# A hybrid attention and recurrence encoder step: bias rows reversed through DRAM instead of by a matmul, wider memsets on GpSimd, and the last softmax scalings on VectorE or ScalarE

## The chip, the cores and the metric

The kernel runs on one core of a Trainium2 chip, in a single launch. The metric is the device time of that launch in microseconds, the median of several runs. The engines are TensorE (PE, matmuls), VectorE (DVE), ScalarE (ACT), GpSimd (POOL) and SyncE (SP, whose queue issues every DMA of this kernel). Each engine works through its own list of instructions in a fixed order and waits for the others by semaphores.

## The reference

One layer of an encoder that has two kinds of heads side by side, for a prompt of 2048 rows and a sample of 64 rows with a cache. One input projection makes eight kinds of features. Four pairs of attention heads use q, k, v and a gate; four recurrent heads use q, f, i and a gate. The attention adds a learned bias by clipped relative distance:

```python
idx = jnp.clip(rel, -REL_CLIP, REL_CLIP) + REL_CLIP          # REL_CLIP = 128
bias = rel_bias[:, idx].astype(jnp.float32)
s = jnp.einsum('bnqhd,bnkhd->bnhqk', q, k).astype(jnp.float32) * ATTN_SCALE + bias
s = jnp.where(valid[None, :, None], s, NEG_INF)
p = jax.nn.softmax(s, axis=-1).astype(v.dtype)
return jnp.einsum('bnhqk,bnkhd->bnqhd', p, v)
```

A chunk of 64 rows attends to itself and the eight chunks before it, so for 128 query rows a tile of bias is 128 x 640 and its entry depends on the difference of column and row alone: each row is the row above it, shifted by one. The first 384 columns all lie beyond the clip and hold one number per head; the last 256 hold the shifted rows. After both branches comes the output projection with the residual and a final norm.

## The kernel before

The rows are cut into four blocks (SUPER): 512, 512 + 64 (the sample), 512 and 512. For every block TensorE runs 32 projection jobs, one per kind and head, of 24 or 48 matmuls `acc<-xh,w` and `acc<-xl,w`: inputs and weights are held as a high and a low part, and three products are summed. Between those matmuls the kernel weaves the attention of the pairs (scores `s`, transposes `tr`, products `pv`), the recurrence of the heads (bank `g`) and, near the end, the output products `acc<-...,slot`. In block 0 each weight is also loaded (`wraw`), split by VectorE and GpSimd into `w` and stored to `wd`, from where the later blocks load it.

The order is not written out by hand. A planner (class Plan, lines 52 to 237) runs the parts of the program as threads at build time and keeps a clock for each engine from a table of costs (Queue.cost, lines 284 to 330). A thread yields what it waits for, a condition, a time, or a time on an engine, and goes on when the planned clock is there. `C.pick(t, D=..., A=...)` names the engine on which work that is ready at t would be done first by those clocks. For SP the planner counts 520 ns from a DMA's start, then its bytes at 370 per ns behind what is already on the way, then 2000 ns and a lag of 100 (lines 204 to 208, 236 to 237, 288). The instructions then stand in that order on each engine whatever the real times are.

The bias of a pair is made once, in block 0, by `load_bias` (line 815), in a single buffer `bias` of 128 x 2 x 640, and stored to `biasd` for the later blocks. A DMA loads a window `ck` in which row p starts at element p of the reversed bias; the rows then run in the wrong direction, so a float32 matmul with the constant `flip` (ones on the other diagonal) turns them over into bank `g`, and VectorE negates the result into `nb[:, :, 384:640]`. VectorE fills the first 384 columns from `far` (`bias<-reset,far`), and two memsets put a large number where a key is not to be seen. The store to `biasd` follows, and `d.bias_at` lets the pair's scores begin (softmax_rows, line 1013). A softmax is: scores on TensorE into the single bank `s`; one custom VectorE instruction that adds the bias and takes the minimum (`pr,nm<-s,bias`, with its row `nm`; the order calls both ISA); the exponential on ScalarE with its sum; a reciprocal; and the scaling of the probabilities. The scaling is on VectorE, except once `parts` is in `have`, which is so only in the last pair of the last block: there it is on ScalarE (line 1049). The probabilities are then transposed and split into `ph`, a high part by ScalarE and a low part by VectorE, for the `pv` products.

GpSimd gets a short memset of `C.breath`, a tile of its own, after three instructions that the planner queued behind one another (lines 261 to 265); its result is not used.

Of the kernel before, what the change touches and what calls it, by code (L numbers as in the profile page):

```python
# [8 lines left out]
F32 = mybir.dt.float32  # L9
# [3 lines left out]
ALU = mybir.AluOpType  # L13
# [4 lines left out]
P = 128  # L18
D = 1024
# [353 lines left out]
def hymba_step(  # L373
# [24 lines left out]
    C = Plan()  # L398
    act, dve, pool, pe, sp = (Queue(C, e, x) for e, x in (("A", nc.scalar), ("D", nc.vector), ("P", nc.gpsimd),
                                                          ("T", nc.tensor), ("S", nc.sync)))  # L400
# [4 lines left out]
    cst = ctx.enter_context(tc.tile_pool(name="cst", bufs=1))  # L405
    wk = ctx.enter_context(tc.tile_pool(name="wk", bufs=2))
    dr = ctx.enter_context(tc.tile_pool(name="dr", bufs=1, space=DRAM))
# [5 lines left out]
    def T(pool_, shape, dt, tag, **kw):  # L413
        uid[0] += 1
        C.name(homes.get(id(pool_), ""), tag, kw.get("bufs") or 1, f"{tag}_{uid[0]}")
        return pool_.tile(list(shape), dt, tag=tag, name=f"{tag}_{uid[0]}", **kw)

    def psum(tag, shape=(P, 512), bufs=1):
        return T(ps, shape, F32, tag, bufs=bufs)
# [22 lines left out]
    def mm32(out, w, x):  # L442
        pe.matmul(out, w, x, start=True, stop=True)

    tk = {k: Tok(C, n) for k, n in dict(acc=2, s_ps=1, tr=2, pv=1, g=1, pr=PRB, ph=2, sig=2, vT=2, mixa=2,
                                     w=WBUFS, raw=RAWB, xn=XNB, kv=1, q=1, sga=2, bias=1, gf=1, gi=1, gg=1,
                                     ck=1, slot=4, x4=0, x5=0, rec=1).items()}
# [1 line left out]

    ident = T(cst, [P, P], F32, "ident")  # L450
    make_identity(nc, ident)
    flip = T(cst, [P, P], F32, "flip")
    ones = T(cst, [P, P], F32R, "ones")
    mask = T(cst, [P, P], U32, "mask")
    eps_t = T(cst, [P, 1], F32, "eps")
    one_t = T(cst, [P, 1], F32, "one")
    C.breath = T(cst, [P, 1], F32, "breath")
    reset = T(cst, [P, 512], F32, "reset")
    asb = [T(cst, [P, 4, P], F32, f"asb{i}") for i in range(2)]
    g_norm = T(cst, [P, NHB], F32, "gnorm")  # L460
# [5 lines left out]
    have = set()  # L466

    def constants():
        pool.memset(eps_t, EPS)
        pool.memset(one_t, 1.0)  # L470
        maskf = asb[0][:, 0]
        pool.memset(maskf, 1.0)
        dve.tensor_copy(ones, maskf)
        pool.memset(flip, 1.0)
        pool.affine_select(out=flip, in_=flip, pattern=[[1, P]], compare_op=ALU.is_equal, fill=0.0,
                           base=-(P - 1), channel_multiplier=1)
        pool.affine_select(out=maskf, in_=maskf, pattern=[[1, P]], compare_op=ALU.is_ge, fill=0.0,
                           base=0, channel_multiplier=-1)
        dve.tensor_copy(mask, maskf)
        pool.memset(reset, 1.0)  # L480
        pool.memset(reset.rearrange("p (b t) -> p b t", t=32)[:, :, 0:1], 0.0)
        pool.memset(asb[0], 0.0)
# [333 lines left out]
    def load_bias(sb, p, d):  # L816
        yield from tk["bias"].get()
        nb = d.bias = T(wk, [P, 2, 640], F32, "bias", bufs=1)
        if sb:
            sp.dma_start(nb, biasd[p])  # L820
            d.bias_at = C.dma(655)
            return
        yield from tk["ck"].get()
        win = T(wk, [P, 4, P], F32, "ck", bufs=1).rearrange("p (h a) c -> p h (a c)", h=2)
        sp.dma_start(win, bass.AP(rel_rev.tensor, 2 * p * 383, [[1, P], [383, 2], [1, 256]]))
        far = T(wk, [P, 2], F32, "far", bufs=1)
        sp.dma_start(far, bass.AP(rel_rev.tensor, 2 * p * 383, [[0, P], [383, 2]]))
        t = C.dma(400)
        yield "D", t
        for h in range(2):  # L830
            dve.tensor_scalar(nb[:, h, 0:384], reset[:, :384], 0.0, far[:, h : h + 1], ALU.mult, ALU.subtract)
        C.dve(600)
        yield from tk["g"].get()
        pw = psum("g")
        pe.matmul(pw, flip, win.rearrange("p h c -> p (h c)"), start=True, stop=True)
        tk["ck"].put()
        t = C.pe()
        yield "D", t
        dve.tensor_scalar(nb[:, :, 384:640], pw.rearrange("p (h c) -> p h c", h=2), -1.0, None, ALU.mult)
        tk["g"].put(1, C.dve())  # L840
        dve.memset(nb[64:128, :, 0:64], BIG)
        dve.memset(nb[0:64, :, 576:640], BIG)
        t = C.dve(900, t)
        d.bias_at = t
        yield t
        sp.dma_start(biasd[p], nb)
        C.dma(655)
# [38 lines left out]
    def pair_jobs(sb, p):  # L886
# [10 lines left out]
        def open_():  # L897

            yield from tk["kv"].get()
            d.kd = T(pa, [P, 2, WIN + NMAX], F32R, "kd")  # L900
            d.v = T(pa, [P, 9, 4, 64], F32R, "v")
            d.q = T(pa, [P, 2, QW], F32R, "q")
            if sb:
                cd = carry[sb - 1][p]
                sp.dma_start(f32(d.kd[:, :, 0:512]), cd[:, 0:2, :])
                sp.dma_start(f32(d.v[:, 0:4].rearrange("p t s d -> p (t s d)")),
                             cd[:, 2:4, :].rearrange("p a c -> p (a c)"))
                d.k_t = d.v_t = C.dma(1024)
            C.spawn(load_bias(sb, p, d), 1)
            if smp:  # L910
                pool.memset(f32(d.v[DEC:, 4 + WIN // P]), 0.0)
                C.spawn(sample_cache(d), 1)
# [98 lines left out]
    def softmax_rows(d, h, qc, spans, bcol, nk, out):  # L1011

        yield lambda: d.q_n >= qc + P and d.k_n >= qc + P and d.bias_at is not None
        yield max(d.q_t, d.k_t, d.bias_at) + 300.0
        yield from tk["s_ps"].get()
        yield from tk["pr"].get()
        sps = s_ps()
        for part in (d.q, ql):
            for i, (k0, kn) in enumerate(spans):
                mm(sps[:, i, :kn], part[:, h, qc : qc + P], d.kd[:, h, k0 : k0 + kn], kn,  # L1020
                   start=part is d.q, stop=part is ql)
        t = C.pe()
        yield "D", t
        s = T(wk, [P, 640], F32, "pr", bufs=PRB)
        nm = T(wk, [P, 2], F32, "nm", bufs=4)
        ns, kn = len(spans), spans[0][1]
        dve.tensor_tensor_reduce(
            s[:, :nk].rearrange("p (a c) -> p a c", a=ns), sps[:, :ns, :kn],
            d.bias[:, h, bcol : bcol + nk].rearrange("p (a c) -> p a c", a=ns),
            1.0, 3e38, ALU.add, ALU.min, nm[:, 0:1])  # L1030
        t = C.dve(nk + 80, t)
        tk["s_ps"].put(1, t)
        d.left -= 1
        if d.left == 0:
            if d.sb == len(SUPER) - 1 and d.p == NPAIR - 1:
                have.add("scores")
                tk["x4"].put()
            tk["bias"].put()
        yield "A", t
        yield from softmax_exp(s, nm, nk, out, t)  # L1040

    def softmax_exp(s, nm, nk, out, t):
        sm = T(wk, [P, 1], F32, "sm", bufs=4)
        act.activation(s[:, :nk], s[:, :nk], AF.Exp, bias=nm[:, 0:1], scale=-1.0, accum_out=sm)
        t = C.act(nk + 300, t)
        yield "D", t
        dve.reciprocal(sm, sm)
        t = C.dve()
        if "parts" in have:
            yield "A", t  # L1050
            act.activation(s[:, :nk], s[:, :nk], AF.Copy, scale=sm)
            t = C.act()
        else:
            dve.tensor_scalar(s[:, :nk], s[:, :nk], sm, None, ALU.mult)
            t = C.dve()
        out.append((s, t))
# [184 lines left out]
    def sample_a(d, c0, marks):  # L1241
# [41 lines left out]
        yield "A", t  # L1283
        out = []
        yield from softmax_exp(s, nm, 576, out, t)
        pr, t = out[0]
        yield lambda: marks[-1]["pv"] and turn["ph"] == turn["given"]
# [749 lines left out]
    def program():  # L2037


        dve.memset(g_in, 0.0)  # L2040
        constants()
        kroom = f32(T(pa, [P, 2, WIN + NMAX], F32R, "kd")).rearrange("p a c -> p (a c)")
        vroom = f32(T(pa, [P, 9, 4, 64], F32R, "v")).rearrange("p t s d -> p (t s d)")
# [252 lines left out]
```

## Time and profile before

| what | us |
|---|---|
| median of 3 runs (1261.01 to 1264.11) | 1261.85 |
| the profiled execution | 1260.86 |
| its span in the trace | 1259.00 |
| TensorE busy in it | 1238.8 |
| VectorE, ScalarE, GpSimd busy | 891.9, 706.9, 379.9 |

The profile is of one execution. Busy time of an engine counts its instructions, not its waits; TensorE's matmuls overlap, so a matmul's own duration is longer than the step from one to the next. A tile's view lists the instructions that write or read it with the shortest, middle and longest duration in ns. A wait row reads: who waited, for whose work on which tile, microseconds in total, times, the longest. A row of the timeline has the start, the length, the engine and the work, and in brackets the idle time just before with what ended it. For a DMA, "to landing" is the time from its issue to the arrival of its last piece.

### The profile page before, as it was taken

How to read it: one execution, taken by the hardware profiler on the slowest of the kernel's cores; microseconds unless marked ns; L12 is line 12 of the kernel's file. 1: busy time of each engine (PE TensorE's matmuls, PEld its weight loads, DVE VectorE, ACT ScalarE, POOL GpSimd, SP SyncE). 2: the span in 40 equal slices, each digit the busy share in tenths (PEclk: the TensorE clock that was granted, in tenths of full speed). 3: DMA queues.
4: the chain of work that ended last, by engine and by line, in shares of the span. 5: the costliest groups of instructions: out<-in, count | busy, mean ns of one | idle time of the engine just before them, and what ended most of it. 6: DMA issues, size and time to landing. Idle time of an engine off the chain costs nothing. (4 is left out here: it accounts for less than half of the span.)

```text
span 1259.0 us, 22201 instructions
## 1 busy us (share of the span) xinstructions
PE 1238.8 (98%) x8120; PEld 1081.6 (86%) x8120; DVE 891.9 (71%) x1854; ACT 706.9 (56%) x1548; POOL 379.9 (30%) x703
## 2 busy tenths in 40 slices
PE   9999999999999999999999999999999999999997
PEld 8788887999999999998888888998888888788786
DVE  7786968766857678686584849783838574578886
ACT  6453546665656557575565656764636454753443
POOL 7766655111120210202533634110101104451110
PEclk9999999999999999999999999999999999999999
DMA  7887787645354554636879597646454657886331
GB/s 288 301 288 244 247 282 281 219 168 202 138 188 142 181 200 144 216 125 236 272 248 303 206 364 254 220 164 210 144 212 136 222 178 279 324 277 203 126 134 67
DMA packets 94830, 271.72 MB, mean 216 GB/s; under 512 B 10305, under 2 KB 43073, under 8 KB 77058
## 3 DMA queue, kind: packets, MB, share of 16 engines
q1 hardware_dynamic: 94722, 270.31, 61.4%
q8 instruction: 64, 1.05, 0.3%
q14 instruction: 44, 0.36, 0.1%
HBM read 186.66 MB, written 83.62 MB: 215 GB/s over the span
## 5 line engine op out<-in xcount | busy, mean ns | idle before, releaser
L266 PE MATMUL acc<-xh,w 128*128 128x512 f32 (+2 forms) x2720 | 568.4, 348 | 1.0 <-ACT sig L266 0.8
L266 PEld LDWEIGHTS acc<-xh,w 128*128 128x128 f32 x2720 | 436.7, 189 | 51.7 <-issue 1.4
L266 PE MATMUL acc<-xl,w 128*128 128x512 f32 (+2 forms) x1360 | 297.4, 348 | 0.0
L266 PEld LDWEIGHTS acc<-xl,w 128*128 128x128 f32 x1360 | 219.3, 189 | 24.9 <-issue 0.5
L266 POOL TENSOR_TENSOR mixa<-mixa,sga 128x256 f32<-128x256 f32 (+1 forms) x36 | 29.8, 828 | 334.8 <-DVE mixa L266 259.6
L266 DVE CUSTOM_DVE_ANT_0 pr<-s,bias 128x640 f32<-128x640 f32 (+5 forms) x144 | 100.7, 703 | 34.5 <-PE s L266 33.9
L266 ACT ACTIVATE pr<-pr,nm 128x640 f32<-128x640 f32 (+4 forms) x132 | 100.7, 763 | 39.0 <-DVE nm L266 37.9
L266 ACT CAST ph<-tr 128x512 fp32r<-128x512 f32 (+3 forms) x176 | 88.1, 507 | 59.7 <-PE tr L266 27.9
L266 POOL TENSOR_TENSOR w<-wraw,w 128x256 fp32r<-128x256 f32 x120 | 105.3, 906 | 46.9 <-DVE w L266 25.9
L266 DVE TENSOR_TENSOR ph<-tr,ph 128x512 fp32r<-128x512 f32 (+3 forms) x176 | 101.1, 589 | 10.0 <-ACT ph L266 8.8
L266 PE MATMUL pv<-ph,v 128*128 128x256 f32 (+2 forms) x344 | 97.2, 373 | 3.1 <-DVE ph L266 2.4
L266 PE MATMUL tr<-ident,pr 128*128 128x128 f32 x580 | 91.2, 273 | 2.4 <-DVE pr L266 1.2
L266 PEld LDWEIGHTS tr<-ident,pr 128*128 128x128 f32 x580 | 70.4, 140 | 16.6 <-issue 3.8
L266 ACT ACTIVATE sig<-acc 128x256 f32<-128x256 f32 (+2 forms) x86 | 42.7, 497 | 73.6 <-PE acc L266 73.3
L266 ACT COPY vT<-acc 128x512 f32<-128x512 f32 (+2 forms) x64 | 31.3, 488 | 71.2 <-PE acc L266 71.1
L266 DVE TENSOR_SCALAR pr<-pr,sm 128x640 f32<-128x640 f32 (+3 forms) x124 | 67.9, 547 | 4.4
L266 DVE TENSOR_TENSOR mixa<-mixa,pv 64x256 f32<-64x256 f32 (+1 forms) x144 | 56.8, 394 | 18.9 <-ACT mixa L266 14.7
L266 PEld LDWEIGHTS pv<-ph,v 128*128 128x128 f32 x344 | 57.4, 190 | 10.3 <-issue 2.0
L266 ACT ACTIVATE sig<-sig 128x512 f32<-128x512 f32 (+2 forms) x109 | 57.3, 528 | 10.0 <-DVE gk L266 7.3
L266 PE MATMUL s<-kd,q 128*128 128x320 f32 (+3 forms) x232 | 56.9, 315 | 0.2
L266 POOL TENSOR_TENSOR xn<-wraw,xn 128x256 fp32r<-128x256 f32 x48 | 37.8, 803 | 62.2 <-ACT xn L266 62.1
L266 PE MATMUL s<-kd,ql 128*128 128x320 f32 (+3 forms) x232 | 55.6, 309 | 0.0
(319 smaller groups left out, 2064.5 us busy)
## 6 DMA issues: line engine op xcount, KB each, us to landing
w<-wd SPq DMA_DIRECT2D x96, 1024.0 KB, 5.1
wd<-w SPq DMA_DIRECT2D x32, 1024.0 KB, 7.6
wraw<-in_w_in_dram SPq DMA_DIRECT2D x30, 512.0 KB, 5.5
wod<-xn SPq DMA_DIRECT2D x28, 512.0 KB, 5.0
xn<-in_x_prompt_dram SPq DMA_DIRECT2D x23, 512.0 KB, 5.5
bias<-biasd SPq DMA_DIRECT2D x12, 640.0 KB, 7.5
carry<-kd SPq DMA_DIRECT2D x12, 512.0 KB, 8.0
carry<-v SPq DMA_DIRECT2D x12, 512.0 KB, 5.2
```

The lines of the kernel that those rows point to most:

```text
L266: r = f(*args, **kw)
```

## The change

It has three parts. In block 0's `load_bias`, the window `ck`, the matmul with `flip` and the bank `g` go. A DMA copies the pair's 766 numbers 128 times into a DRAM tile `rel`, one copy after another (the 128 copies are the outermost dimension of both sides). The thread yields until 3000 ns after the planned landing; a second DMA then loads rows from `rel` with a step of 765 where a row has 766, so that each row starts one element earlier, straight into the bias buffer. VectorE fills the far columns as before and negates the loaded part in place, at the planned landing plus 500 ns. Second, `breath` is 128 x 128 instead of 128 x 1. Third, the late scaling goes to ScalarE only where the planner's clocks favour it.

```diff
-    flip = T(cst, [P, P], F32, "flip")
...
-    C.breath = T(cst, [P, 1], F32, "breath")
+    C.breath = T(cst, [P, P], F32, "breath")
...
-        pool.memset(flip, 1.0)
-        pool.affine_select(out=flip, in_=flip, pattern=[[1, P]], compare_op=ALU.is_equal, fill=0.0,
-                           base=-(P - 1), channel_multiplier=1)
...
-        yield from tk["ck"].get()
-        win = T(wk, [P, 4, P], F32, "ck", bufs=1).rearrange("p (h a) c -> p h (a c)", h=2)
-        sp.dma_start(win, bass.AP(rel_rev.tensor, 2 * p * 383, [[1, P], [383, 2], [1, 256]]))
+        same = T(dr, [P, 2 * 383], F32, f"rel{p}")
         far = T(wk, [P, 2], F32, "far", bufs=1)
         sp.dma_start(far, bass.AP(rel_rev.tensor, 2 * p * 383, [[0, P], [383, 2]]))
-        t = C.dma(400)
+        t = C.dma()
+        sp.dma_start(same, bass.AP(rel_rev.tensor, 2 * p * 383, [[0, P], [1, 2 * 383]]))
+        yield C.dma() + 3000.0
+        near = nb[:, :, 384:640]
+        sp.dma_start(near, bass.AP(same.tensor, same.offset + P - 1, [[2 * 383 - 1, P], [383, 2], [1, 256]]))
+        tn = C.dma(400)
         yield "D", t
         for h in range(2):
             dve.tensor_scalar(nb[:, h, 0:384], reset[:, :384], 0.0, far[:, h : h + 1], ALU.mult, ALU.subtract)
-        C.dve(600)
-        yield from tk["g"].get()
-        pw = psum("g")
-        pe.matmul(pw, flip, win.rearrange("p h c -> p (h c)"), start=True, stop=True)
-        tk["ck"].put()
-        t = C.pe()
-        yield "D", t
-        dve.tensor_scalar(nb[:, :, 384:640], pw.rearrange("p (h c) -> p h c", h=2), -1.0, None, ALU.mult)
-        tk["g"].put(1, C.dve())
+        yield "D", tn + 500.0
+        dve.tensor_scalar(near, near, -1.0, None, ALU.mult)
...
-        if "parts" in have:
+        if "parts" in have and C.pick(t, D=680.0, A=780.0) == "A":
```

Since the planner lays the order anew, instructions move on every engine, most in block 0. Three places matter to the prediction. The first is SP's list at the first pair of block 0. Before:

```order
L266 DMA wraw_580<-in_w_in_dram 128x1024
L266 DMA wd_35_107<-w_484 128x2048
L266 DMA ck_596<-in_rel_bias_dram 128x2x256
L266 DMA far_598<-in_rel_bias_dram 128x2x1
L266 DMA wraw_685<-in_w_in_dram 128x1024
L266 DMA wd_39_111<-w_609 128x2048
```

And in the changed kernel, from the same place:

```order
L266 DMA far_590<-in_rel_bias_dram 128x2x1
L266 DMA rel_152_589<-in_rel_bias_dram 128x766
L266 DMA wraw_678<-in_w_in_dram 128x1024
L266 DMA wd_38_110<-w_604 128x2048
L266 DMA wraw_713<-in_w_in_dram 128x1024
L266 DMA wd_42_114<-w_661 128x2048
L266 DMA bias_588<-rel_152_589 128x2x256
```

The load of the bias rows now stands two weights later, behind a store of 1 MB. At pairs 1 to 3, too, weights' transfers or two to three loads of x stand between the copy and the load.

The second place is VectorE's list at the same pair. Before, from the bias to the next weight's split:

```order
L266 TENSOR_SCALAR bias_595<-reset_80,far_598 128x384 x2
L266 TENSOR_TENSOR sga_727<-acc_600,sig_700 128x512
L266 CAST w_732<-wraw_685 128x1024
L266 TENSOR_TENSOR q_180_739<-k_181_740,q_179_738 128x512
L266 TENSOR_SCALAR bias_595<-g_745 128x2x256
L266 MEMSET bias_595 64x2x64 x2
L266 CAST w_784<-wraw_729 128x1024
```

In the changed kernel, the end of the same stretch:

```order
L266 TENSOR_TENSOR kd_585<-vT_795,kd_585 64x512 x2
L266 TENSOR_TENSOR q_179_740<-k_180_741,q_178_739 128x512
L266 TENSOR_SCALAR bias_588<-bias_588 128x2x256
L266 MEMSET bias_588 64x2x64 x2
L266 TENSOR_TENSOR v_586<-tr_847,v_586 128x4x128
L266 ISA pr_871,nm_872<-s_866,bias_588 128x128
```

The negation has moved behind the splits of q and k, next to the first scores' min-reduction. On TensorE those scores now read:

```order
L266 MATMUL s_866<-kd_585,q_587 128x128
L266 MATMUL s_866<-kd_585,ql_157 128x128
L266 MATMUL acc_834<-xl_156,w_733 128x512 x4
L266 MATMUL s_880<-kd_585,q_587 128x256
L266 MATMUL s_880<-kd_585,ql_157 128x256
```

Four projection matmuls stand between the first two groups of scores, which share bank s; before, there were four as well.

The third place is VectorE's list in the last pair of the last block, about the residual add into `xn` that follows the sum `asb`. Before:

```order
L266 RECIPROCAL sm_13026<-sm_13026 128x1
L266 TENSOR_TENSOR asb_9_81<-asb_9_81,acc_13010 128x512
L266 RECIPROCAL sm_13031<-sm_13031 128x1
L266 TENSOR_TENSOR xn_12951<-xn_12951,acc_13041 128x512
L266 TENSOR_TENSOR ph_13060<-tr_12980,ph_13060 128x256
L266 TENSOR_TENSOR ph_13066<-tr_12998,ph_13066 128x512
```

In the changed kernel:

```order
L266 RECIPROCAL sm_13014<-sm_13014 128x1
L266 TENSOR_SCALAR pr_12990<-pr_12990,sm_13014 128x640
L266 RECIPROCAL sm_13026<-sm_13026 128x1
L266 TENSOR_SCALAR pr_13016<-pr_13016,sm_13026 128x640
L266 TENSOR_TENSOR mixa_12908<-mixa_12908,pv_12955 64x256 x2
L266 TENSOR_SCALAR b_2550_13039<-ss_13037 128x1
L266 TENSOR_TENSOR asb_8_80<-asb_8_80,acc_13019 128x512
L266 TENSOR_TENSOR ph_13061<-tr_12999,ph_13061 128x512
L266 TENSOR_TENSOR ph_13067<-tr_13009,ph_13067 128x512
L266 TENSOR_TENSOR xn_12936<-xn_12936,acc_13051 128x512
```

The scalings stand on VectorE, all eight of the last pair, and none of them is left on ScalarE; two subtractions for `ph` now stand ahead of the add into `xn`. On GpSimd the memsets of breath are 37 instead of 36, and six half-width additions and subtractions near the end have become three whole ones on VectorE.

## The prediction

> **What bounds the kernel now.** I read the page's head first, then TensorE's waits, then a table by stage, then the places of the change.
>
> ```profile
> span 1259.0 us, 22201 instructions
> PE 1238.8 (98%) x8120; PEld 1081.6 (86%) x8120; DVE 891.9 (71%) x1854; ACT 706.9 (56%) x1548; POOL 379.9 (30%) x703
> ...
> PEclk9999999999999999999999999999999999999999
> ```
>
> TensorE is busy for 98% of the span, at full granted clock in every slice; no other engine passes 71%. The time is therefore the length of TensorE's own instruction list plus its gaps. The table by stage shows where those are; the first number after the comma is TensorE's busy time.
>
> ```profile
> 40.00:280.00 240.00, 235.62 (x1544) 200.22 (x1545) 187.31 (x382) 126.32 (x273) 121.19 (x175) 1.00 0.72 251
> 280.00:1040.00 760.00, 757.04 (x5401) 680.52 (x5400) 521.71 (x1168) 452.56 (x990) 167.86 (x379) 1.00 0.59 205
> 1040.00:1120.00 80.00, 77.63 (x384) 64.33 (x383) 42.72 (x87) 44.88 (x88) 39.70 (x65) 1.00 0.79 290
> 1120.00:1259.00 139.00, 131.94 (x566) 104.71 (x564) 109.96 (x171) 59.24 (x147) 20.57 (x20) 0.99 0.46 150
> ```
>
> From 40 to 280 us, where block 0 runs and the change does most, TensorE idles 240.00 - 235.62 = 4.38 us; from 1040 to 1120 us, the last pair's attention, 80.00 - 77.63 = 2.37 us. No reordering there can bring more than these 6.75 us. What can bring more is to take work out of TensorE's list. The waits of TensorE over the run, and then its matmuls around the second flip:
>
> ```profile
> PE pv L266 <- DVE ph L266: 2.4, 2, 1.4
> ...
> PE tr L266 <- DVE pr L266: 1.2, 1, 1.2
> ...
> PE g L266 <- DVE bias L266: 0.9, 2, 0.4
> ```
>
> ```profile
> 106.27 1.64 PE L266 MATMUL acc<-xh,w 128*128 128x512 f32 x6
> 107.74 1.02 PE L266 MATMUL g<-ck,flip 128*128 128x512 f32 x2
> 108.20 1.03 PE L266 MATMUL acc<-xh,w 128*128 128x512 f32 x2
> 109.07 1.53 PE L266 MATMUL acc<-xl,w 128*128 128x512 f32 x6
> 111.04 0.70 PE L266 MATMUL g<-q,ones 128*128 128x512 f32 x2 [0.44 <-DVE bias L266]
> ...
> 165.84 1.02 PE L266 MATMUL g<-ck,flip 128*128 128x512 f32 x2
> 166.30 1.03 PE L266 MATMUL acc<-xh,w 128*128 128x512 f32 x2
> 167.17 1.53 PE L266 MATMUL acc<-xl,w 128*128 128x512 f32 x6
> 169.14 0.70 PE L266 MATMUL g<-q,ones 128*128 128x512 f32 x2 [0.44 <-DVE bias L266]
> ```
>
> ```profile
> 1132.69 27.88 PE acc L266 x119
> ```
>
> **The flips removed.** The chain's row gives the pace of a 512-column projection matmul: 27.88 / 119 = 0.234 us. From the start of a flip to the start of the xl group lie 109.07 - 107.74 = 1.33 us, and 167.17 - 165.84 = 1.33 us. Two projection matmuls of that are 0.47; one flip costs 0.86 us of TensorE, four cost **-3.44 us**. They stand in a list that is never empty, so all of it comes off the end.
>
> The flip also holds bank g until VectorE has negated it, and the norm's ones matmul wants that bank. Six projections from 109.07 end at 110.47; the ones matmul starts at 111.04, 0.57 us late. At the third flip it is 169.14 - (167.17 + 1.40) = 0.57. With no flip nothing holds the bank: **-1.14 us**.
>
> **The bias through DRAM.** The window load (256 KB, one hop) gives way to a copy of 392 KB from DRAM to DRAM and a load of 256 KB that SP may issue only once the copy has landed.
>
> ```profile
> L266 DVE TENSOR_SCALAR bias<-reset,far x8: 408/418/940, 48.4 to 234.9; 128x384 f32<-128x384 f32 x8
> L266 DVE MEMSET bias<- x8: 165/165/165, 54.1 to 237.0; 64x128 f32 x8
> L266 DVE TENSOR_SCALAR bias<-g x4: 679/685/692, 53.3 to 236.0; 128x512 f32<-128x512 f32 x4
> ```
>
> ```profile
> L266 SPq DMA_DIRECT2D ck<-in_rel_bias_dram x4: 423/430/438, 36.7 to 229.1; - x4
> ...
> DMA to landing us min/median/max: 3.5/4.2/8.4
> ```
>
> ```profile
> carry<-kd SPq DMA_DIRECT2D x12, 512.0 KB, 8.0
> ...
> biasd<-bias SPq DMA_DIRECT2D x4, 640.0 KB, 5.1
> ```
>
> No copy within DRAM is in this trace; its nearest rows by size and by destination are the stores to biasd (5.1 us) and carry (8.0). I take 6. The code issues the load 3 us after the landing it plans, which is 0.52 + 392/370 + 2.1 us after the issue (the planner's numbers, microseconds and bytes per ns): in all 6.7 us. So SP stands at the load for at most about 1.3 us, behind it the next weight loads and stores; SP's own waits show room for that:
>
> ```profile
> SPq L266 <- PE acc L266: 291.5, 73, 10.1
> ```
>
> I cost SP's stand at nothing; the cover is weights asked for ahead, and without it the 1.3 us would come four times, 5.2.
>
> VectorE's side is different. The load's rows are those of the old window load, same bytes and pieces: 3.5, 4.2, 8.4 us. The code allows 0.52 + 256/370 + 2.1 + 0.5 = 3.8 us, so it lands 0.3 early, 0.4 late or 4.6 late. Then VectorE stops at its in-place negation, with the rest of its list behind it, and in the new order the first scores' min-reduction follows two or three instructions later. Before, the bias was far ahead of its use:
>
> ```profile
> 53.31 0.68 DVE L266 TENSOR_SCALAR bias<-g 128x512 f32<-128x512 f32 x1
> ...
> 65.64 0.29 DVE L266 CUSTOM_DVE_ANT_0 pr<-s,bias 128x128 f32<-128x128 f32 x1 [0.71 <-PE s L266]
> ```
>
> From the negation's end at 53.99 to the first min-reduction at 65.64 lie over 11 us; the change uses this cushion up. The second scores matmul cannot start before the first min-reduction has freed bank s, and it stands only four projections, 0.94 us, behind the first. I let the median lateness reach TensorE at each of four pairs: **+1.6 us**, with ends 0 and +18.4 (four times 4.6); an early landing starts nothing sooner on an engine that has no gap to fill. I choose the median since only one of the four, the first, was as late as 8.4:
>
> ```profile
> DMA to landing us min/median/max: 8.4/8.4/8.4
> ```
>
> (the same view, cut to 30 to 60 us). The scores of block 0 also move later in TensorE's list, between other projections; its content stays. What such a shift can lose or win I bound by the stage's 4.38 us of idle time, either way, and take zero.
>
> The negation itself moves from PSUM (685 ns) to SBUF; the nearest row, a scaling of the same shape, is below at 620 ns. Four times 0.07 beside other work: nothing.
>
> **Late scaling.** In the last pair eight scalings go from ScalarE to VectorE; the order shows that the choice by clocks gives VectorE all eight.
>
> ```profile
> L266 DVE TENSOR_SCALAR pr<-pr,sm 128x640 f32<-128x640 f32 x88 | 51.2, 582 | 3.1
> ...
> L266 ACT ACTIVATE pr<-pr,sm 128x640 f32<-128x640 f32 x8 | 6.5, 826 | 1.9 <-DVE sm L266 1.9
> ...
> L266 DVE TENSOR_SCALAR pr<-pr,sm 128x512 f32<-128x512 f32 x8 | 5.0, 620 | 0.3
> ```
>
> VectorE gains 8 x 0.582 = 4.7 us and ScalarE loses 8 x 0.826 = 6.6, in a stage where VectorE is busy 42.72 of 80 us and ScalarE 44.88: room on both. The two waits of pv for ph in the waits above (2.4 us) lie in this stage. In one, VectorE stands at a residual add while two ph subtractions wait behind it:
>
> ```profile
> 1087.38 0.15 DVE L266 RECIPROCAL sm<-sm 128x1 f32<-128x1 f32 x1
> 1090.20 0.69 DVE L266 TENSOR_TENSOR xn<-xn,acc 128x512 f32<-128x512 f32 x1 [2.66 <-ACT asb L266]
> 1090.80 1.01 DVE L266 TENSOR_TENSOR ph<-tr,ph 128x256 fp32r<-128x256 f32 x2
> ```
>
> The new order puts ph ahead of xn there. Ends: all 2.4 gone, or as much again added by 4.7 us of VectorE work; I take half the gain, **-1.2 us**.
>
> **Longer memsets.**
>
> ```profile
> L266 POOL MEMSET breath<- x36: 88/98/642, 23.0 to 1112.7; 128x1 f32 x36
> ```
>
> ```profile
> L266 POOL MEMSET flip<- x1: 204/204/204, 1.5 to 1.5; 128x128 f32 x1
> ```
>
> The 128x128 memset of flip took 204 ns, so 36 of them add 36 x 0.106 = 3.8 us to GpSimd, spread over the run; it is busy 30%. Ends: a loss of 3.8 if each reached TensorE, a gain of 1.2 if the pauses let VectorE through in a third of the three waits on ph and pr (3.6 us). I take zero.
>
> The Trainium skill, SBUF — State Buffer, section "Who interferes with whom", says that VectorE and GpSimd hold a shared port pair for a whole instruction, and that a GpSimd instruction which only writes leaves two-input VectorE instructions alone but still shuts out VectorE's two-port forms. The trace agrees that something shuts VectorE out at times: fills of one shape took 408 and 940 ns. By that rule a longer memset helps subtractions and hurts scalings; it is the fourth rival below.
>
> **Sum.** -3.44 - 1.14 + 1.6 - 1.2 + 0 = **-4.2 us**. The profiled execution took 1260.86 us, its span 1259.00; 1256.7 by it. It lies 1.0 under the median of 1261.85, so in medians **1257.7**.
>
> **Rivals.**
> 1. *The landing decides, slower.* If the second load lands as late as the slow ones, VectorE stops at four negations and TensorE behind it. Without the late gain the sum is -4.6 + 4 x lateness; it passes +3.8 us (0.3%) when the landing exceeds 3.8 + 2.1 = 5.9 us. At 6.3 us it gives +5.4: 1267.3; at 8.4, +13.8: 1275.7. For: at the first pair the load stands right behind a 1 MB store in SP's list, as the window load did that took 8.4, and the DMA engines are busy 0.72 of that stage. Against: half of the four loads took 4.2 or less, and VectorE waited for the far rows, which travel with them, only this much:
>
> ```profile
> DVE bias L266 <- DMA far<-in_rel_bias_dram: 1.2, 2, 1.0
> ```
>
>  Chance 0.20.
> 2. *The gain is given back, 1261.7.* Lateness near 1.1 us per pair (landing 4.9) returns the 4.6, or the new interleaving of blocks 0 to 2 brings as many waits as it loses. Chance 0.15.
> 3. *Waits go too, 1251.7.* All idle time of the two stages goes, bank g's share counted once: 3.44 + 6.75 = 10.2. The negations would have to be on time everywhere. Chance 0.10.
> 4. *The pauses hurt, 1261.5.* VectorE is at times shut out while GpSimd works (a fill of 940 ns for 408), and if the longer memsets do so too, their 3.8 us reach TensorE: -4.2 + 3.8. Against: GpSimd is idle in most of the run. Chance 0.05. The shared-pair rule cited above would have this happen to scalings and fills.
>
> A copy confined to few DMA engines would be a form of rival 1. The Trainium skill, DMA: Bandwidth & Descriptors, section "Why a DMA increments its semaphore by 16 and not by 1", lets the slowest dimension set the engine count; here that is 128, so by it the copy uses all sixteen. No row of this trace shows it.
>
> **Chances.** The forecast holds 0.50, with its own range 1254.0 to 1260.0; two thirds of that lie below 1258.1. A difference under 0.3%, 3.8 us, is about what a measurement cannot tell from none. Faster: 0.33 + 0.10 = 0.43; same: 0.17 + 0.15 + 0.05 = 0.37; slower 0.20. The range 1253.0 to 1265.5 leaves out about half of rival 3 and two thirds of rival 1.
>
> **What would show it.** No g matmul from ck and eight matmul records fewer; the two 0.44 us waits for the bias gone; idle of VectorE before the four negations, released by the DMA into bias, under 1 us each (right) or over 2 (rival 1), with TensorE idle just behind; no pv wait of over 1 us between 1040 and 1120 us; GpSimd up by under 4 us with TensorE's other waits as they were. I am wrong if TensorE's idle time from 40 to 280 us passes 8 us, or if its busy time does not fall by about 3.4.

## The result and the profile after

| what | before | after |
|---|---|---|
| median us, measured side by side, 6 runs each | 1261.53 | 1249.35 |
| ratio, 95% interval | | 0.9901 [0.988, 0.9922] |
| the profiled execution, us | 1260.86 | 1249.03 |
| its span, us | 1259.00 | 1247.0 |

One of the six runs of after took 2041.33 us at a granted clock of 0.557; it is left out of the ratio. The change brings 1.0%, about 12.5 us, where 4.2 were forecast: faster than the low end of the range.

The head of the profile of after:

```profile
span 1247.0 us, 22165 instructions
PE 1231.1 (99%) x8112; PEld 1081.3 (87%) x8112; DVE 886.5 (71%) x1865; ACT 700.5 (56%) x1540; POOL 370.9 (30%) x696
```

TensorE's list is shorter by the eight records of the flips, but its busy time fell by 7.7 us, from 1238.8 to 1231.1. The flips were to take 3.4 of that, so some of the matmuls that are still there seem to have become shorter too. The table by stage for after, cut as in the prediction:

```profile
40.00:280.00 240.00, 237.82 (x1582) 205.54 (x1583) 185.41 (x388) 131.13 (x287) 119.79 (x188) 1.00 0.73 260
280.00:1040.00 760.00, 756.74 (x5390) 680.11 (x5389) 517.32 (x1170) 451.16 (x985) 165.14 (x370) 1.00 0.59 205
1040.00:1120.00 80.00, 79.51 (x389) 66.37 (x388) 53.90 (x102) 42.12 (x92) 40.18 (x63) 1.00 0.91 324
```

Idle time of TensorE from 40 to 280 us went from 4.38 to 2.18 us, from 1040 to 1120 us from 2.37 to 0.49. The waits of TensorE in after:

```profile
PE g L266 <- DVE asb L266: 1.0, 3, 0.5
...
PE pv L266 <- DVE ph L266: 0.5, 1, 0.5
```

The rows of g for the bias and of tr for pr are gone, the row of pv for ph fell from 2.4 to 0.5. One more gain is in no row of waits. The last rows of the chain, which are the output products alone, in before and then in after:

```profile
1132.69 27.88 PE acc L266 x119
1179.78 28.10 PE acc L266 x120
1210.68 41.77 PE acc L266 x180
```

```profile
1096.28 53.77 PE acc L266 x236
1169.26 27.55 PE acc L266 x120
1199.53 40.93 PE acc L266 x180
```

The last 180 matmuls are the same in both kernels, of the same form, with no wait between them, at a granted clock of 1.00 in every slice of 10 us that they fill. They took 41.77 / 180 = 232 ns each before and 40.93 / 180 = 227 ns after. Nothing in the diff touches them.

What the prediction feared did not come. VectorE at the first pair in after, with SP's rows of the copy and the load, and then SP's load and VectorE's negation at pairs 2, 3 and 4 (rows in between left out):

```profile
37.47 1.06 SPq L266 DMA_DIRECT2D rel<-in_rel_bias_dram  x1
...
48.53 0.43 SPq L266 DMA_DIRECT2D bias<-rel  x1
...
62.22 0.69 DVE L266 TENSOR_TENSOR q<-k,q 128x512 fp32r<-128x512 f32 x1
62.83 0.42 DVE L266 TENSOR_SCALAR bias<-bias 128x512 f32<-128x512 f32 x1
63.34 0.41 DVE L266 MEMSET bias<- 64x128 f32 x2
...
67.56 0.28 DVE L266 CUSTOM_DVE_ANT_0 pr<-s,bias 128x128 f32<-128x128 f32 x1
...
118.23 0.38 SPq L266 DMA_DIRECT2D bias<-rel  x1
124.75 0.90 DVE L266 TENSOR_SCALAR bias<-bias 128x512 f32<-128x512 f32 x1
179.35 0.48 SPq L266 DMA_DIRECT2D bias<-rel  x1
195.80 0.41 DVE L266 TENSOR_SCALAR bias<-bias 128x512 f32<-128x512 f32 x1
236.90 0.54 SPq L266 DMA_DIRECT2D bias<-rel  x1
246.93 0.42 DVE L266 TENSOR_SCALAR bias<-bias 128x512 f32<-128x512 f32 x1
```

No bracket stands behind any of the four negations: VectorE did not wait. From the load's issue to the negation lie 62.83 - 48.53 = 14.3 us at the first pair, 124.75 - 118.23 = 6.5 us at the second, and 16.4 and 10.0 us at the third and fourth, where the prediction allowed 3.8. The landings of copy and load together in after, and then those of the load at the first two pairs alone:

```profile
DMA to landing us min/median/max: 3.7/7.6/9.6
```

```profile
DMA to landing us min/median/max: 8.3/8.3/8.3
...
DMA to landing us min/median/max: 5.9/5.9/5.9
```

At the first pair the load had 6.0 us to spare, at the second 0.6. At the third and fourth it took 8.3 and 3.7 us and had 8.1 and 6.3 to spare. The 0.6 us are not safe: in e10, the same kernel again, the load of the second pair took 7.5 us, and VectorE's waits have this row:

```profile
DVE bias L266 <- DMA bias<-rel: 0.4, 1, 0.4
```

### The profile page after: what moved, and what is told of

The parts are those of the page before. It is cut to its first block, busy times and chain, and to the rows that moved or that the text cites. A ratio compares the mean times of both kernels' runs of the same rounds, so it can differ in the third digit from the quotient of the medians.

```text
span 1247.0 us, 22165 instructions
## 1 busy us (share of the span) xinstructions
PE 1231.1 (99%) x8112; PEld 1081.3 (87%) x8112; DVE 886.5 (71%) x1865; ACT 700.5 (56%) x1540; POOL 370.9 (30%) x696
## 4 chain that ended last, share of the span: by engine, by line
PE 86%; DVE 5%; issue 2%; DMA 2%; POOL 2%; ACT 2%; SPq 0%; DVEq 0%; POOLq 0%; ACTq 0%
PE acc L266 62%; PE g L266 8%; PE tr L266 6%; PE s L266 5%; PE pv L266 5%; POOL w L266 1%; DVE xn L266 1%; DMA So<-in_state_hgrn_dram 1%; DMA wd<-w 1%; DVE pr L266 1%; DMA xn<-in_x_prompt_dram 1%; ACT ck L266 0%; DVE q L266 0%; DVE xl L266 0%; DVE mixa L266 0%
## 5 line engine op out<-in xcount | busy, mean ns | idle before, releaser
L266 DVE TENSOR_SCALAR pr<-pr,sm 128x640 f32<-128x640 f32 (+4 forms) x132 | 71.8, 544 | 4.7
L266 POOL TENSOR_TENSOR k<-ob 128x512 f32<-128x512 f32 (+2 forms) x20 | 18.3, 915 | 127.3 <-ACT ob L266 117.2
```

The lines of the kernel that those rows point to most:

```text
L266: r = f(*args, **kw)
```

## The experiments

My theory after this comparison: three gains as predicted (flips, bank, late waits), no loss at the gate (the wait that puts the negation off until the load is planned to have landed), and one gain that I had not seen: removing `flip` and widening `breath` moves other tiles in SBUF, and a matmul's step depends on where its two operands lie. The rivals: the output products are faster for a reason of order or of the late scalings; the longer memsets do something on the chip; the gate was never worth anything.

In the built programs each small tile takes a multiple of 32 bytes of a partition. `flip` gave back 512, `breath` took 512 in place of 32. All tiles that are allocated after `breath` on the left side (`reset`, `w`, `xh`, `xl`, `q`, `kd`, `pr`, `ph`) so moved by -32 bytes; `slot`, allocated from the right end, stayed. `w` begins at byte 161280 in before and 161248 in after, `slot` at 210912 in both. In the table, "distance" is (start of slot - start of w) modulo 512 bytes; `xh`, `xl`, `kd`, `q`, `ql` and `v` share it with `w`, and the columns' pieces of 128 float32 are steps of 512 bytes. Modulo 512, distances of 480 and 32 are 32 bytes from 0 on either side, 448 is 64 and 416 is 96. The step is the mean of the last 180 matmuls, from each kernel's chain, and the time is from the ratio to before. It is a mean of unlike pairs of operands: 104 of the 180 read `slot` and one of those tiles, 16 read `slot` and `ph` (96 apart in before, 128 in after), 24 read `slot` and `b11`, which move together and are 0 apart in every kernel here, and in 36 both operands lie on the left. So at most 120 of the 180 changed their distance.

| kernel | order of before? | distance | last 180, us | mean step, ns | ratio to before |
|---|---|---|---|---|---|
| before | yes | 480 | 41.77 | 232.1 | 1 |
| e11, 64 bytes | yes | 416 | 41.77 | 232.1 | 1.0008 [0.9999, 1.0016] |
| e16, 448 bytes by a longer `breath` | yes | 32 | 41.71 | 231.7 | 1.0001 [0.9992, 1.0011] |
| e1, 32 bytes | yes | 448 | 41.30 | 229.4 | 0.9977 [0.9967, 0.9987] |
| e6, slot moved | yes | 448 | 41.30 | 229.4 | 0.998 [0.9971, 0.9988] |
| e9, 480 bytes | yes | 0 | 40.93 | 227.4 | 0.9981 [0.9972, 0.999] |
| after | no | 0 | 40.93 | 227.4 | 0.9901 [0.988, 0.9922] |
| e2, after + 32 bytes | no | 480 | 41.78 | 232.1 | 0.9923 [0.9911, 0.9935] |

**e1: a 32-byte tile into before.**

```diff
+    T(cst, [P, 8], F32, "pad")
     reset = T(cst, [P, 512], F32, "reset")
```

> The kernel before with one unused tile of 32 bytes ahead of reset: every instruction and its order stay, but w, xh, kd, q, ph and pr start 32 bytes higher, as in the changed kernel (modulo 64). Theory 'phase': TensorE's step of a 512-column matmul is about 233 ns where the two operands start in different halves of 64 bytes and 227 where in the same; the output products (some 670) fall from 232 to 227, so 2.5 to 3.5 us less than before, about 1258.5. Rival 'order': the shorter step came from the new order of work (fewer collisions), so 0.0 us, step stays at 232.

Measured: 1260.54 us, 2.9 us less (interval 1.6 to 4.2), not one instruction changed. The step fell to 229.4, only a little over half of the way:

```profile
1210.78 41.30 PE acc L266 x180
```

**e6: slot moved instead.** The same distance from the other side, by a 32-byte tile behind `rest` in the pool of the right side.

```diff
-        more.append(lambda: T(pw, [P, 512], F32, "rest"))
+        more.append(lambda: (T(pw, [P, 512], F32, "rest"), T(pw, [P, 8], F32, "pad"))[0])
```

> The kernel before with an unused tile of 32 bytes at the end of the late pool: slot and b11 start 32 bytes lower, so in the same half of 64 bytes as w, xh and kd are in the kernel before; nothing else moves, the order is the same. Theory 'phase' (it is the two operands' difference that counts): step 227, 2.5 to 3.5 us less than before, about 1258.5. Rival 'place' (w, xh and kd must themselves start at 32): step stays at 232, 0.0 us. Rival 'order': 0.0 us.

Measured: 1260.8 us, 2.5 us less, the same 41.30 us for the last 180. The place of `w` is that of before, the place of `slot` is not: what counts is the distance, not an address.

**e2: the changed kernel, moved back.** The pad of e1 in after.

> The changed kernel with one unused tile of 32 bytes ahead of reset, which puts w, xh, kd, q, ph and pr back where they were modulo 64; the order is that of the changed kernel. Theory 'phase': the output products' step goes back to 232, 2.5 to 3.5 us more than the changed kernel, about 1252.3. Rival 'order': as the changed kernel, 1249.3.

Measured: 1253.75 us, ratio 0.9923 against after's 0.9901, so about 2.8 us over after, though the two intervals overlap. The step is before's 232.1, in after's order.

**e9: all of after's places in before's order.** The pad of e1 with 120 columns in place of 8.

> The kernel before with an unused tile of 480 bytes ahead of `reset`: every instruction and the order are those of before, and slot and the operands to the left of it now start at the same place modulo 512 bytes, as in the changed kernel (in before they stand 32 bytes apart, in e1 64 bytes apart, modulo 512). Theory A (the step of a matmul is set by the distance of its two operands' starts, on a scale finer than 512 bytes, and 64 bytes apart is only half a cure): the output products step at 227 to 228 ns as in the changed kernel, where e1 had 229.6; 517 slot matmuls x about 5 ns = 2.6 us less than before, ratio near 0.9975, and TensorE's waits unchanged. Rival B (only the place modulo 64 bytes counts, and what the changed kernel has beyond e1 comes from its order): 229.6 ns as in e1, about 1.4 us less.

Theory A held: the chain of e9 ends with after's 40.93 us.

```profile
1134.08 27.37 PE acc L266 x119
1180.65 27.56 PE acc L266 x120
1210.93 40.93 PE acc L266 x180
```

The time fell by 2.4 us (1.3 to 3.5); the three groups of output products are 0.51, 0.54 and 0.84 us shorter than in before, 1.9 together. By time e1 and e6 gained as much with half of the step; intervals of this width do not tell half from whole, the steps do. So the layout is worth 2.4 us of the 12.5, and e1's half step is explained by the distance of 64 bytes, not by an order.

**e11: the control.** The pad with 16 columns, 64 bytes.

> The kernel before with an unused tile of 64 bytes ahead of `reset`: the left tiles move by twice as much as in e1, and slot stands 96 bytes from the operands to its left, modulo 512. If the distance decides (odd multiples of 32 bytes bad, 64 half, 0 good): 232 to 233 ns, before's time within 0.5 us. If any shift of the tiles, or more room at this place, does what e1 did: 229.6 ns or less.

Measured: 1262.9 us, as before (ratio 1.0008), and before's chain:

```profile
1132.65 27.92 PE acc L266 x119
1179.80 28.13 PE acc L266 x120
1210.72 41.77 PE acc L266 x180
```

A shift as such does nothing. In these kernels an odd multiple of 32 bytes goes with a mean step of 231.7 to 232.1 ns, 64 bytes with 229.4, a distance of 0 with 227.4.

**e3: the bias through DRAM alone**, in before; the late scaling and `breath` are as before, and the places give the distance of before.

> The kernel before with the bias rows through DRAM alone (flip gone, short memsets, late scaling on ScalarE; places modulo 64 as before). My sum of the prediction: 3.4 for the flips, 1.1 for the bank, 1.6 lost to the landing, so about 2.9 us less, 1258.6. Theory 'bias brings more': what block 0 gained in the changed kernel's trace (about 6 us by 285 us) is all this part, so about 6 us less, 1255.5. Rival 'memsets or choice': part of the 6 us is theirs, so 3 to 4.5 us less.

Measured: 1256.11 us, ratio 0.995 [0.9937, 0.9963]: 6.3 us less (4.7 to 7.9), and before's 2.4 us of pv for ph is still there:

```profile
PE pv L266 <- DVE ph L266: 2.4, 2, 1.4
```

In the traces the last 180 matmuls start 5.2 us earlier than in before. TensorE's busy time is 1235.4 us, 3.4 less than before's 1238.8, which is what the flips were to take. The prediction's terms without the gate make 4.58.

**e13: e3 with four float32 matmuls put back.** The result of the four is not used, and nothing waits for it.

```diff
+        yield from tk["g"].get()
+        pe.matmul(psum("g"), ident, reset[:, :512], start=True, stop=True)
+        tk["g"].put(1, C.pe())
         yield "D", tn + 500.0
```

> e3 (the bias through DRAM alone) with one float32 matmul of 128x512 on bank g put back at each of the four pairs; its result is not used, and nothing holds the bank behind it. If a flip costs TensorE what the prediction read (0.86 us), the four give back 3.4 of the 6.3 us that e3 gained: about 2.9 us below before, ratio 0.9977. If most of e3's gain came from the new order and the float32 matmul costs less than that in the list: 4.5 us or more below before.

Measured: 1258.48 us, ratio 0.9969 [0.9957, 0.998], 3.9 us below before. The four matmuls take back 2.4 of e3's 6.3 us, and TensorE's busy time rises by 4.6, from 1235.4 to 1240.0. The planner laid the order of e13 anew, each ratio is uncertain by some 1.5 us, and the busy time of four traces of after's own order runs from 1230.5 to 1232.4 (after, e10, e15, e17). So 3.4 lies between the two readings, and neither a smaller price with a larger share of the order nor a larger price is excluded.

**e12: the gate opened.** In the changed kernel the negation is not put off to the planned landing.

```diff
-        yield "D", tn + 500.0
         dve.tensor_scalar(near, near, -1.0, None, ALU.mult)
```

> The changed kernel, with the negation of the loaded bias rows and the two memsets put straight behind the fills of the far columns, eight instructions earlier in VectorE's list, instead of at the planned landing. VectorE must now stand at the load of the bias rows at each of the four pairs. As the prediction priced such a stand, all of what the load still needs reaches TensorE: about 4 us at each pair, 16 us in all, slower than before. Rival: the negation stands so far ahead of its use (two banks of projections are already filled) that VectorE stops 2 to 4 us at each pair, and TensorE loses less than 4 us in all; then even a late landing could not have given the change back.

Measured: 1268.65 us, ratio 1.006 [1.0048, 1.0073]; the changed kernel beside it (e10, below) had 1250.38, so 18.3 us more. Not all of this need be the gate's: without its wait the planner lays another order on every engine, so the comparison has the stands and the new order together. VectorE's own waits, and its first and third negations, in e12:

```profile
DVE bias L266 <- DMA bias<-rel: 27.9, 4, 9.5
```

```profile
58.96 0.43 DVE L266 TENSOR_SCALAR bias<-bias 128x512 f32<-128x512 f32 x1 [7.10 <-DMA bias<-rel]
...
195.20 0.43 DVE L266 TENSOR_SCALAR bias<-bias 128x512 f32<-128x512 f32 x1 [9.50 <-DMA bias<-rel]
```

It stood 27.9 us at four pairs. TensorE in e12, over block 0 and in the two slices at its end:

```profile
40.00:280.00 240.00, 225.20 (x1429) 190.05 (x1429) 181.97 (x363) 122.65 (x261) 121.62 (x189) 0.97 0.71 253
240.00:250.00 10.00, 1.83 (x4) 1.16 (x4) 7.06 (x12) 4.87 (x12) 2.65 (x6) 0.62 0.58 182
250.00:260.00 10.00, 9.26 (x56) 9.06 (x57) 4.66 (x11) 4.14 (x10) 0.00 (x0) 0.70 0.29 86
```

TensorE idled 14.8 us of the 240, 12.6 more than in after. Most of it did not come at the pairs but near 240 us, in two stops, one for ph and one for vT; in the slices there the granted clock was 0.62 and 0.70, and TensorE's busy time over the run is 1237.4 us, where after has 1231.1 and e10 1232.4. The two stops:

```profile
244.33 1.83 PE L266 MATMUL pv<-ph,v 128*128 128x512 f32 x4 [5.21 <-DVE ph L266]
250.46 1.22 PE L266 MATMUL acc<-xh,w 128*128 128x256 f32 x4 [4.31 <-ACT vT L266]
```

Whether and through which buffers the stands of the first three pairs reach that place I did not separate. The rival in this expectation, less than 4 us in all, is not what came. The 16 us came near, but by luck in part: the expectation put them at the four pairs, and most of TensorE's idle time came elsewhere.

**e5: the choice for the late scalings alone**, in before.

> The kernel before with the changed choice for the late scalings alone; all places modulo 512 bytes as before. If the choice alone takes away the two long waits of pv for ph in the last pair (2.4 us in before), the time falls by 2 to 2.4 us, ratio 0.998, with idle time of TensorE from 1040 to 1120 us near 0.5 us as in the changed kernel. If the waits went because the changed bias or the longer memsets shifted the order there, it stays within 0.5 us of before and the 2.4, 2 row is still there. The prediction had -1.2.

Measured: 1259.87 us, ratio 0.9979 [0.997, 0.9988], 2.6 us less (1.5 to 3.8). The late stage and the wait in e5:

```profile
1040.00:1120.00 80.00, 78.93 (x396) 65.91 (x395) 48.99 (x98) 42.62 (x87) 40.70 (x66) 1.00 0.84 303
```

```profile
PE pv L266 <- DVE ph L266: 1.1, 1, 1.1
```

TensorE's idle time there fell from 2.37 to 1.07 us, so 1.3 of the 2.6 us can be pointed at.

**e7: the changed kernel without the choice.**

> The changed kernel with the late scalings on ScalarE always, as before; places as in the changed kernel. If the choice is what took the late waits away: waits of pv for ph of over 1 us come back and the time is 2 to 2.5 us over the changed kernel's (1251.5 where that has 1249.35), ratio to before near 0.992. If something else did, the time is the changed kernel's within 0.5 us, ratio near 0.990.

Measured: 1251.37 us, ratio 0.9915 [0.9902, 0.9929]. The wait is back:

```profile
1040.00:1120.00 80.00, 77.30 (x378) 64.20 (x377) 43.19 (x83) 44.06 (x89) 44.45 (x68) 1.00 0.86 307
```

```profile
PE pv L266 <- DVE ph L266: 2.5, 2, 1.5
```

Idle time of that stage is 2.70 us against 0.49 in after, 2.2 more. The medians (1251.37 against 1249.35, or 1250.38 in another group) agree in sign, but their intervals overlap.

**e4: longer memsets alone**, 128x120 in before, at an odd multiple of 32 bytes as before.

> The kernel before with the longer memsets of `breath` alone (128x120, so that the places of the other tiles keep a distance of an odd multiple of 32 bytes from slot, as in before). If longer memsets do nothing but move the tiles: before's time within 1 us, output products at 232 to 233 ns. If the pauses let VectorE through: 1 to 2 us less, with smaller waits for ph and pr. If they hold it back: up to 3.8 us more. The prediction had 0.

Measured: 1259.78 us, ratio 0.9986 [0.9977, 0.9995]: 1.8 us less (0.6 to 2.9).

**e8: the changed kernel with 128x1 memsets** in a tile of the same size.

> The changed kernel with the memsets of `breath` again 128x1, in a tile that keeps its 512 bytes, so that all places stay as in the changed kernel. If the longer memsets did something only through the places of the other tiles: the changed kernel's time within 0.5 us (ratio to before near 0.990), GpSimd's busy time about 4 us lower. If the pauses let VectorE through: 0.5 to 1.2 us slower than the changed kernel, with more waits for ph and pr. If the pauses held VectorE back: faster by up to 3.8 us.

Measured: 1252.56 us, ratio 0.9931 [0.9911, 0.9951], slower than after in median by some 2 to 3 us, though the intervals overlap.

**e14: 128x256 memsets**, with e10, the changed kernel again, beside it.

> The changed kernel with `breath` 128x256, twice as long; it moves the other tiles by 512 bytes, so that their places modulo 512 bytes stay. GpSimd is busy about 4 us more. If the length of the memsets itself does the good that e8 lost (about 2 us), this is as fast as the changed kernel or up to 1 us faster. If what e8 lost came from another order alone, it can go either way by 1 to 2 us, and the rows of waits show other places.

> The changed kernel once more, unaltered, so that the others of this group stand beside it on one chip. Near 0.990 of before.

Measured: e14 1253.04 us, ratio 0.9937 [0.9923, 0.9951]; e10 1250.38 us, ratio 0.9913 [0.99, 0.9927]. Short and long memsets are both slower in median than the 128x128 ones, by 2 to 3 us, but the intervals overlap. In e4, e8 and e14 the planner lays another order, since it charges a memset by its length. The next three hold the order of every engine to the last instruction and change only the length on the chip, for instance:

```diff
-    C.breath = T(cst, [P, P], F32, "breath")
+    C.breath = T(cst, [P, P], F32, "breath")[:, 0:3]
...
-                return 95.0 + 0.85 * n, 60.0, False
+                return 95.0 + 0.85 * (P if n == 3 else n), 60.0, False
```

**e15: after's order, 128x3; e17: after's order, 128x256; e16: before's order, 128x120.**

> The changed kernel in exactly its own order on every engine and with its places, but the memsets of `breath` write 128x3 (the planner still charges them as 128x128). If the length of a memset does something on the chip (VectorE gets through, or is held back, while GpSimd pauses), the time moves by 0.5 to 4 us from the changed kernel's. If the memsets acted only by the order that the planner lays for them, it stays within 0.5 us, ratio to before near 0.991.

> The same with memsets of 128x256 (charged as 128x128; places modulo 512 bytes as in the changed kernel). By the order alone: the changed kernel's time within 0.5 us, where e14, whose order moved too, lost 2.3. By length: the opposite of what e15 shows.

> The kernel before in exactly its own order, with memsets of 128x120 (charged as 128x1; slot at an odd multiple of 32 bytes from its partners as in before). By the order alone: before's time within 0.5 us, where e4, whose order moved too, gained 1.7. By length: the gain of e4 is here as well.

Measured: e15 1250.38 us, 0.9915 [0.9898, 0.9931]; e17 1249.13 us, 0.9906 [0.9888, 0.9924]; e16 1263.26 us, 1.0001 [0.9992, 1.0011]. The memsets in after, e15 and e17:

```profile
L266 POOL MEMSET breath<- x37: 194/203/756, 22.7 to 1101.2; 128x128 f32 x37
```

```profile
L266 POOL MEMSET breath<- x37: 90/100/108, 24.5 to 1102.4; 128x3 f32 x37
```

```profile
L266 POOL MEMSET breath<- x37: 302/311/317, 22.6 to 1101.8; 128x256 f32 x37
```

From 100 to 311 ns a memset, and the time does not move by more than the runs scatter. Between e8 and e15, both with short memsets, the planner's charge differs and with it the order. Nor does e4's gain come with the length: e16, of the same length and at the same places but in before's order, gains nothing (the two intervals overlap only from 0.9992 to 0.9995). So what the longer memsets brought did not come from their length; what is left is the order that their charge led to.

## Why the prediction was too small, step by step

The three gains that it named show in the rows that it named. What failed were two terms: the +1.6 for the bias load's lateness, and the zero for the edit of `breath`, in which neither the places of the tiles (2.4 us) nor the order that the planner lays by a memset's charge (1.8 us) was thought of. With the first alone put right, the sum would still have been only -5.8 us. Of the signs that it named, VectorE's idle time before the negations and the waits of pv came as written; GpSimd's busy time, which was to rise by under 4 us, fell by 9.0 (379.9 to 370.9), and TensorE's fell by 7.7 in place of 3.4.

**Flips, -3.44: the direction shown, the size within what was measured.** The records are gone, and e3's busy time of TensorE is 3.4 us below before's; with four such matmuls put back (e13) 2.4 us of the 6.3 went.

**Bank g, -1.14.** The two 0.44 us waits are gone from after's rows. It was not tried apart from the flips.

**The bias load's lateness, +1.6: this step failed, and it was the one with the wrong sign.** It put the negation 3.8 us behind the load's issue, from the code's constants. That is only the time of an empty queue. The planner counts a DMA's bytes behind those on the way, and the thread goes on when VectorE's planned clock gets there; the rows of after give 14.3, 6.5, 16.4 and 10.0 us. The other numbers of the step were also off, and in the other direction. The load's landing, taken at 4.2 from the old window's rows, was 8.3, 5.9, 8.3 and 3.7. The price of a stand is open: the step let each microsecond of it reach TensorE, and e12, with stands of 27.9 us, took 18.3 us longer, but in another order and mostly at another place than the pairs. So rival 1 described a real danger, and it was its condition that did not hold: the landing did exceed 5.9 us at two pairs, but the time allowed was not 3.8. At the second pair that was close, with 0.6 us to spare in after and a wait of 0.4 in e10. SP's own stand at the copy, put at nothing, was nothing: the copies took 5.9 to 9.6 us to land, where 6 was assumed, but the loads were issued 11.1 to 12.1 us after them, not 6.7, and no row of SP's waits in after names `rel`.

**Order of block 0, taken as zero.** Idle time of TensorE there fell by 2.2 us (4.38 to 2.18), twice the bank's share. That is no accident of one trace: six traces of before's order have 4.0 to 5.5 us there, five of after's 2.0 to 3.0, and e3 has 2.5. e3 gained 6.3 [4.7, 7.9] against 4.58 by these terms; whether the order gave the rest or the runs' scatter is open.

**Late scaling, -1.2: right mechanism, too small.** All 96 scalings of this shape are now on VectorE, as the group's row of after shows, and the wait fell to 0.5, not to half:

```profile
L266 DVE TENSOR_SCALAR pr<-pr,sm 128x640 f32<-128x640 f32 x96 | 54.6, 569 | 3.4
```

Alone it gave 2.6 us (1.5 to 3.8), with 1.3 us less idle time in that stage; in the changed kernel the idle time fell by 1.9. The end of -2.4 in the prediction was the better value.

**Longer memsets, 0: right on the chip, wrong as an account of the edit.** e15, e16 and e17 show that their length does nothing that can be measured, so the fourth rival is refuted; the rule cited beside it (the Trainium skill, SBUF — State Buffer, "Who interferes with whom") has no price here that these runs can see. But the edit does two things that no duration shows. Its charge moves the planner's order (e4: -1.8), and its tile, together with the removal of `flip`, moves every later tile by 32 bytes (e9: -2.4). The second was in neither the sum, the rivals nor the range.

The four parts measured alone (e3 -6.3, e9 -2.4, e5 -2.6, e4 -1.8) make -13.1, beside -12.5 measured; each is uncertain by 1 to 1.6, so the sum closes only within some 3 us. Against the forecast, the error of about 8 us splits into the gate (1.6), the layout (2.4), the order by the memsets' charge (1.8), the late stage (1.4) and what the bias gave beyond its terms (1.7), together 8.9, which is within the same scatter. None of the variants tried is faster than the changed kernel beyond the scatter.

## What to carry to other kernels

Removing or resizing a small constant can move every tile allocated after it: before pricing such an edit by time alone, compare where the operands of the busiest matmuls begin before and after. Where TensorE's list is always full, a change of some ns in one matmul's step is not visible in any wait; look for it in the pace of a stretch whose instructions did not change. A planned time read off constants is a bound for an empty queue, so read the distance from issue to use off the order or the trace, and test the price of a gate by opening it, with the order held if that can be done.

## What the runs showed of the hardware that I had not expected

The mean step of the last 180 matmuls of 128x512 (f32 in the rows), in a full list at a granted clock of 1.00, is 227.4, 229.4 or 231.7 to 232.1 ns where `slot` and the tiles on the left start 0, 64 or an odd multiple of 32 bytes apart, modulo 512 (before, e1, e6, e9, e11, e16, e2). Moving either side has the same effect. Since at most 120 of the 180 changed their distance, my estimate for one of those is about 7 ns between an odd multiple of 32 bytes and none (41.77 - 40.93 = 0.84 us over 120). Why it matters was not shown, and no larger distance was tried apart. Also, when TensorE stopped for 5.2 and 4.3 us within 12 us, its granted clock in the two slices of 10 us there was 0.62 and 0.70, and 1.00 in the next ones.
